# ScalarE writes a residual into PSUM, one block's addition stands first, and GpSimd forms three low parts instead of four

## The chip, the cores and the metric

The kernel runs on one core of a Trainium2 chip. The core has TensorE (matrix products, into PSUM), VectorE and ScalarE (elementwise work, on SBUF and PSUM), GpSimd (elementwise work, on SBUF only), and DMA queues that SyncE and others issue. The metric is the device time of one execution in microseconds; a timed figure is the median of several executions. In the profile the engines are called PE (matmul), PEld (weight load), DVE (VectorE), ACT (ScalarE), POOL (GpSimd) and SP (SyncE); a letter q behind a name is that engine's queue.

## What is computed

One decoder layer in float32 on 256 tokens of width 1024: a mixer of causal pooling and block attention, cross-attention into 256 memory tokens, and a dense SwiGLU layer, each followed by a layer norm over a scaled residual. The change lies in the last step, which is

```
h = layer_norm(DEEPNORM_ALPHA * h + swiglu(h, w_gate, w_up, w_down), ln3_g, ln3_b)

def swiglu(h, w_gate, w_up, w_down):
    return (jax.nn.silu(h @ w_gate) * (h @ w_up)) @ w_down      # w_down: 2816 x 1024

def layer_norm(x, g, b):
    mu = jnp.mean(x, axis=-1, keepdims=True)
    var = jnp.mean(jnp.square(x - mu), axis=-1, keepdims=True)
    return (x - mu) * lax.rsqrt(var + 1e-5) * g + b
```

with DEEPNORM_ALPHA = 2 ** 0.25.

## The kernel before

**High and low parts.** Every float32 operand of a product is split in two: a high part rounded to a format that TensorE takes at full pace (`hi`), and the low part, what is left (`lo = raw - hi`). A product is then three matmuls: high by high, high by low, low by high. For a weight tile of 128x1024, ScalarE makes the high part (a cast) and VectorE the low part (a subtraction of two SBUF tiles). For the tiles whose numbers stand in `ws.helped`, GpSimd makes the low part (line 163).

**The weight stream.** `Stream` holds a list of items in the order in which TensorE uses them. An item is a weight tile from DRAM ("whole"), a pair made from sums of weight blocks ("sums"), or a tile that stands in SBUF already ("home"). Each call of `get` ticks the stream, and a tick prepares at most the next item, up to 9 items (`AHEAD`) past those that TensorE is done with. The order of the items is therefore the order in which casts and low parts enter ScalarE's, VectorE's and GpSimd's queues. Each of these queues runs in order.

**The down projection.** The product with `w_down` is taken in 11 chunks of 256 rows. Ten of them (0 to 9) use a seven-product form for 2x2 blocks: tokens are halved into two blocks of 128, columns into halves of 512, and the 256 rows into two blocks of 128. For these chunks TensorE accumulates

- four shared products `p1`, `p5`, `p6`, `p7`, each in a PSUM bank of its own (`shared_products`);
- products that go straight into the block of the result that needs them: `C11` (token block 0, left half) and `C12` (token block 0, right half) in `four`, and `C21` (token block 1, left half) in `fourth`. The weights of a fourth product are a sum of weight blocks that was put aside earlier in a home of SBUF (`t4`); one home holds the fourth weights of two neighbouring chunks.

Chunk 10 (weight rows 20 and 21, `rest`) is multiplied in the plain way into every block at the end.

The shared products are merged on the way out (`merge`): `merged[0]` is a copy of `p1` by ScalarE (line 1268), and VectorE forms `merged[4] = merged[0] + p6` (line 1269), `merged[1] = merged[4] + p5` for `C12` (1272), `merged[2] = merged[4] + p7` for `C21` (1275) and `merged[3] = merged[2] + p5` for `C22`, token block 1's right half (1278). `C22`, the lower right block, has no straight product; it is `merged[3]`, the residual `ALPHA * h2` and the plain chunk. It is kept in two parts of 256 columns, (1, 512, 768) and (1, 768, 1024), in two banks.

**The end of the kernel.** The function `down` is a generator; each `yield` ends one step of TensorE's work. A dictionary of events puts other engines' work between the steps: at steps 16 to 19 one step each of `merge`. After the last `four`, `down` loads the scale and shift of the last norm (`load_norm`, lines 1290 and 1291), prepares what is left of the stream, and then puts on VectorE's queue, in this order: the two parts of `C22` (line 1299, residual and `merged[3]` in one instruction with two SBUF inputs and a PSUM output), and the addition of `merged[1]` into `C12` (line 1301). TensorE then goes through the pieces: the plain chunk into `C11`, into `C12` (which needs line 1301), into the first part of `C22` (which needs line 1299), then the fourth products of chunks 4 to 7 and 0 to 3 (items 137 to 140, whose low parts GpSimd makes), then the plain chunk into the second part of `C22` and into the two halves of `C21`. For the latter VectorE first adds `merged[2]` (line 1371).

VectorE meanwhile norms token block 0 (lines 1332 to 1351) and begins token block 1. On GpSimd's queue stand, in order, the low parts, the power that makes the reciprocal deviation of token block 0 (line 865), two additions of the shift `b` (line 1350), and the power for token block 1.

**Homes and tags.** The four homes `t4[0]` to `t4[3]` and the norms' buffers come from one pool, in which a tag has a fixed number of slots. Tag `r` has two slots and serves the norms' row buffers; tags `g` and `b` have one slot each and serve the norm's scale and shift. Before, homes 0 and 1 lie in `r`, home 2 in `g`, home 3 in `b`. So the load of the last scale waits until home 2 is split, the load of the last shift until home 3 is, and the last norm's row buffers wait for homes 0 and 1.

Of the kernel before, what the change touches and what calls it, by code (L numbers as in the profile page):

```python
# [11 lines left out]
OP = mybir.AluOpType  # L12
# [3 lines left out]
D = 1024  # L16
# [17 lines left out]
PR_BUFS = 7  # L34
BUSY = 7
SEVEN, LAG, PAIRED, ASIDE = 10, 2, 8, 9
GROUPED = 3


# [171 lines left out]
def decoder_layer(  # L211
# [56 lines left out]
    def row(k):  # L268

        return w_down[k * P:(k + 1) * P].rearrange("(k p) n -> p k n", p=P)  # L270
# [3 lines left out]
    def t4_home(c):  # L274

        if c // 2 not in t4:
            tag, bufs = (("r", 2), ("r", 2), ("g", None), ("b", None))[c // 2]
            t4[c // 2] = nmp.tile([P, 1, D], F32, name=f"t4{c // 2}", tag=tag, **({"bufs": bufs} if bufs else {}))
        return t4[c // 2][:, :, c % 2 * 512:(c % 2 + 1) * 512]

# [17 lines left out]
    def add_low(n):  # L298
        c_low[n] = ws.add(row(2 * n + 1), 1)
# [3 lines left out]
    for n in range(PAIRED):  # L303
        add_low(n)
        if n == 5:
            add_sums(ASIDE)
            add_fourth(ASIDE)
            add_low(ASIDE)
    c_dn = {c: [ws.add(row(2 * c + f), 1) for f in range(2)] for c in range(SEVEN, NFC)}
    for n in (4, 6, 0, 2):  # L310
        add_fourth(n)
    ws.helped.update(c_t4[n][0] for n in (4, 6, 0, 2))


    xt = ap.tile([P, T, D], F32, tag="a8", name="xt")
# [944 lines left out]
    def merge():  # L1260

        p1, p5, p6, p7 = shared

        def u(i):
            return sp.tile([P, 512], F32, name=f"u{i}", tag="pr", bufs=PR_BUFS)

        merged.update({n: u(n) for n in (0, 4)})
        nc.scalar.copy(merged[0], p1)
        nc.vector.tensor_add(merged[4], merged[0], p6)  # L1269
        yield  # L1270
        merged[1] = u(1)
        nc.vector.tensor_add(merged[1], merged[4], p5)  # L1272
        yield
        merged[2] = u(2)
        nc.vector.tensor_add(merged[2], merged[4], p7)  # L1275
        yield
        merged[3] = u(3)
        nc.vector.tensor_add(merged[3], merged[2], p5)  # L1278

    def down():  # L1280

# [13 lines left out]
        acc[1, EDGE, D] = bank("acc")[:, :D - EDGE]  # L1295
        ws.prepare(ws.used + AHEAD)
        ws.held = True
        for c0, c1 in ((512, EDGE), (EDGE, D)):
            nc.vector.scalar_tensor_tensor(acc[1, c0, c1], h2[:, 1, c0:c1], ALPHA, merged[3][:, c0 - 512:c1 - 512],  # L1299
                                           op0=OP.mult, op1=OP.add)  # L1300
        nc.vector.tensor_add(acc[PIECES[1]], merged[1], acc[PIECES[1]])  # L1301
        for piece in (*PIECES[:2], (1, 512, EDGE), (1, EDGE, D), (1, 0, CUT), (1, CUT, 512)):
            t, c0, c1 = piece
            if piece == (1, EDGE, D):
                for c in (4, 6, 0, 2):
                    yield from fourth(c, c + 2)
                yield "left"
            for j, numbers in enumerate(rest):
                y_hi, y_lo = pair(get(done + j), ALL, slice(t * P, (t + 1) * P))
                hi, lo = [w[:, c0:c1] for w in ws.get(numbers, 0)]  # L1310
                end = j == len(rest) - 1
                nc.tensor.matmul(acc[piece], y_hi, hi, start=False, stop=False, skip_group_check=True)  # L1312
                nc.tensor.matmul(acc[piece], y_hi, lo, start=False, stop=False, skip_group_check=True)  # L1313
                nc.tensor.matmul(acc[piece], y_lo, hi, start=False, stop=end, skip_group_check=True)  # L1314
                yield
            yield piece
# [3 lines left out]
        0: lambda: fourth_split(4, PAIRED), 3: lambda: gated_split(ASIDE), 4: lambda: gated_in(NFC - 1),  # L1320
        5: lambda: token_sums_split(ASIDE, aside), 13: lambda: gated_split(NFC - 1),
    }
    events.update({step: lambda: run(parts, 1) for step in (16, 17, 18, 19)})
    for step in range(22):
        events.get(step, lambda: None)()
        run(dn, 1)
# [120 lines left out]
```

## Time and profile before

| | us |
|---|---|
| median of 3 runs | 371.55 |
| lowest, highest | 370.69, 371.56 |
| the profiled execution's own time | 370.8 |
| its span (first to last instruction) | 369.0 |
| TensorE busy | 359.5 (97%) |
| VectorE busy | 316.4 (86%) |
| ScalarE busy | 204.8 (55%) |
| GpSimd busy | 76.8 (21%) |

A timeline row of the profile gives the start and the duration of an instruction in us, the engine, the line of the program, the operation, its output and inputs by the program's names, the shapes, and in brackets how long the engine had been idle and what released it. `w135h` and `w135l` are the high and low part of item 135. A row of several instructions (x2) gives the time from the first one's start to the last one's end. Two instructions of one engine overlap a little, so the distance from start to start is what one of them costs; ends of matmuls are modelled, and their distance from start to start is the better measure.

### The profile page before, as it was taken

The numbers are of one execution on the slowest core, as the hardware profiler recorded it, in microseconds if no ns is written. First come the engines' busy times: TensorE is split into PE (matmuls) and PEld (weight loads), VectorE is DVE, ScalarE is ACT, GpSimd is POOL, SyncE is SP. The second block draws the span as 40 slices with busy tenths as digits, with TensorE's granted clock in tenths as the row PEclk, the third lists the DMA queues.
The fourth block names the chain that finished last, engine by engine and source line by source line (L and its number), as shares of the span: only waits on it lengthen the run. The fifth ranks groups of instructions, "written<-read, shape, count | busy, mean of one in ns | idle before, by whom it ended". The sixth has DMA issues, their size and how long they took to land. (4 is left out here: it accounts for less than half of the span.)

```text
span 369.0 us, 5457 instructions
## 1 busy us (share of the span) xinstructions
PE 359.5 (97%) x1840; PEld 306.6 (83%) x1840; DVE 316.4 (86%) x480; ACT 204.8 (55%) x323; POOL 76.8 (21%) x92
## 2 busy tenths in 40 slices
PE   9999999999999999999999999999999999999495
PEld 8887888888888999988888888888888888888384
DVE  5878999985999888575979989999999999799955
ACT  5867776366342864463164564665475465659211
POOL 1000009200000004300100114422430341210940
PEclk9999999999999999999999999999999999999879
DMA  7996388699936978753009879877986886881311
GB/s 231 417 421 272 116 304 329 188 339 343 363 128 236 398 285 290 254 183 124 0 27 339 290 259 312 282 266 269 324 300 229 326 258 236 267 272 24 111 49 68
DMA packets 35771, 89.75 MB, mean 243 GB/s; under 512 B 4256, under 2 KB 14112, under 8 KB 35616
## 3 DMA queue, kind: packets, MB, share of 16 engines
q1 hardware_dynamic: 34688, 87.57, 67.3%
q0 software_dynamic: 624, 1.57, 1.3%
q8 instruction: 14, 0.23, 0.2%
q10 hardware_dynamic: 432, 0.26, 0.2%
q14 instruction: 13, 0.11, 0.1%
HBM read 82.05 MB, written 7.34 MB: 242 GB/s over the span
## 5 line engine op out<-in xcount | busy, mean ns | idle before, releaser
L1116 POOL TENSOR_TENSOR sraw<-gr 128x128 f32<-128x128 f32 x10 | 8.2, 820 | 103.3 <-DMA gr<-gd 68.9
L865 POOL TENSOR_TENSOR rs<-mv,mhalf 128x1 f32<-128x1 f32 x6 | 4.4, 732 | 71.1 <-DVE mv L863 71.1
L718 POOL TENSOR_TENSOR win<-upad 128x271 f32<-128x271 f32 x4 | 3.5, 881 | 52.7 <-DVE upad L752 52.7
L1117 POOL TENSOR_TENSOR sraw<-sraw,gr 128x128 f32<-128x128 f32 x10 | 12.1, 1212 | 0.8
L493 ACT CAST h2Th<-tp 128x512 fp32r<-128x512 f32 x4 | 2.3, 586 | 14.5 <-PE tp L504 14.5
L1096 ACT ACTIVATE sg<-pg 128x256 f32<-128x256 f32 x22 | 7.9, 380 | 2.8 <-PE pg L391 2.8
L494 DVE TENSOR_TENSOR gTl<-gr,gTh 128x512 fp32r<-128x512 f32 x11 | 8.3, 757 | 0.6 <-ACT gTh L493 0.6
L517 POOL DMA_DIRECT2D xd<-xs x3 | 1.9, 628 | 33.3 <-DVE xs L514 33.3
L1118 POOL TENSOR_TENSOR sraw<-gr 128x128 f32<-128x128 f32 x10 | 8.5, 851 | 0.0
L1097 DVE TENSOR_TENSOR sg<-sg,pg 128x256 f32<-128x256 f32 x22 | 8.4, 415 | 0.1
L525 POOL DMA_DIRECT2D xr<-xd x12 | 6.6, 561 | 8.7 <-DMA xd<-xs 6.4
L493 ACT CAST gTh<-gr 128x512 fp32r<-128x512 f32 x11 | 6.8, 614 | 2.8 <-DMA gr<-gd 2.8
L493 ACT CAST S<-sraw 128x384 fp32r<-128x384 f32 (+1 forms) x10 | 5.3, 533 | 5.3 <-POOL sraw L1118 5.3
L622 ACT ACTIVATE pr<-pr,mx 128x256 f32<-128x256 f32 (+1 forms) x12 | 5.5, 461 | 4.5 <-DVE mx L668 4.5
L622 ACT ACTIVATE xpr<-xs,mx 128x256 f32<-128x256 f32 x8 | 3.7, 470 | 7.4 <-DVE mx L633 7.4
L514 DVE STREAM_TRANSPOSE gs<-sg 128x512 f32<-128x512 f32 x11 | 7.7, 702 | 0.1
L1349 ACT ACTIVATE r<-r,rs 128x512 f32<-128x512 f32 x2 | 1.3, 716 | 11.4 <-POOL rs L865 11.4
L1121 POOL TENSOR_TENSOR S<-gr,sraw 128x128 f32<-128x128 f32 x8 | 7.6, 951 | 0.0
L1312 PE MATMUL acc<-w135h,gTh 128*128 128x256 f32 (+1 forms) x6 | 2.5, 420 | 4.8 <-DVE acc L1301 4.8
L870 DVE SCALAR_TENSOR_TENSOR r<-r,mv,g 128x512 f32<-128x512 f32 (+1 forms) x10 | 7.0, 728 | 0.2
L163 POOL TENSOR_TENSOR w137l<-t,w137h 128x1024 fp32r<-128x1024 f32 x1 | 4.0, 4037 | 14.4 <-ACT w137h L162 14.4
L494 DVE TENSOR_TENSOR S<-sraw,S 128x384 fp32r<-128x384 f32 (+1 forms) x10 | 5.8, 578 | 1.3 <-ACT S L493 1.3
(1400 smaller groups left out, 1436.3 us busy)
## 6 DMA issues: line engine op xcount, KB each, us to landing
gd<-gs SPq DMA_DIRECT2D x11, 256.0 KB, 5.8
gr<-gd SPq DMA_DIRECT2D x44, 64.0 KB, 2.0
pd<-ps SPq DMA_DIRECT2D x4, 384.0 KB, 4.2
pt<-pd SPq DMA_DIRECT2D x16, 96.0 KB, 5.3
g<-in_ln_g SPq DMA_DIRECT2D x3, 512.0 KB, 5.0
b<-in_ln_b SPq DMA_DIRECT2D x3, 512.0 KB, 7.3
wr<-in_w_qkv SPq DMA_DIRECT2D x5, 256.0 KB, 4.7
mr<-in_mem_t SPq DMA_DIRECT2D x1, 1024.0 KB, 11.7
```

The costliest lines, as they stand in the source:

```text
L493: nc.scalar.copy(h, ps)
L494: nc.vector.tensor_sub(l, ps, r32(h))
L514: nc.vector.transpose(st[:, :, at:at + m, :].rearrange("p j m b -> p m j b"), src.rearrange("p m (j b) -> p m j b", b=32))
L525: queue.dma_start(raw[32 * j:32 * (j + 1)].rearrange("p i m b -> p i (m b)"), via[:, j, :].rearrange("(i a) r -> a i r", i=4))
L622: nc.scalar.activation(dst[:, j, :], src[:, j, :], AF.Exp, bias=mx[:, j:j + 1], scale=sign, accum_out=sm[:, j:j + 1])
L870: nc.vector.scalar_tensor_tensor(r, r, self.mv[:, 0:1], gb["g", self.i][:, s], op0=OP.subtract, op1=OP.mult)
L1096: nc.scalar.activation(sg, ps[:, :CW].rearrange("p (f b) -> p f b", f=2), AF.Silu, bias=0.0, scale=1.0)
L1097: nc.vector.tensor_mul(sg, sg, ps[:, CW:].rearrange("p (f b) -> p f b", f=2))
L1116: nc.gpsimd.tensor_add(s1, a21, a22)
L1117: nc.gpsimd.tensor_sub(s2, s1, a11)
L1118: nc.gpsimd.tensor_sub(s3, a11, a21)
L1121: nc.gpsimd.tensor_sub(s4_raw, a12, s2)
```

## The change

Four things change together.

- The homes swap tags: home 0 lies in `b`, home 1 in `r`, home 2 in `g`, home 3 in `r`.
- The stream's order: the fourth weights of chunks 4 and 5 (home 2) come ahead of weight rows 20 and 21, and those of homes 0, 1 and 3 behind them, in this order. Only these three are in `ws.helped`. VectorE makes the low part of the first one.
- The two parts of `C22` no longer come from one fused instruction of VectorE. ScalarE multiplies the residual by ALPHA and writes it into the two banks, and VectorE adds `merged[3]` to each in place.
- VectorE's order: `merged[1]` is added to `C12` first; then `merged[2]` and `merged[3]` are formed (before, at steps 18 and 19), then `merged[3]` is added to the two parts of `C22`. TensorE takes the fourth products of chunks 4 and 5 between the plain chunk into `C12` and that into the first part of `C22`; the other three pairs keep their place ahead of the second part.

```diff
+LATE = 4, 0, 2, 6
...
-            tag, bufs = (("r", 2), ("r", 2), ("g", None), ("b", None))[c // 2]
+            tag, bufs = (("b", None), ("r", 2), ("g", None), ("r", 2))[c // 2]
...
+    add_fourth(LATE[0])
     c_dn = {c: [ws.add(row(2 * c + f), 1) for f in range(2)] for c in range(SEVEN, NFC)}
-    for n in (4, 6, 0, 2):
+    for n in LATE[1:]:
         add_fourth(n)
-    ws.helped.update(c_t4[n][0] for n in (4, 6, 0, 2))
+    ws.helped.update(c_t4[n][0] for n in LATE[1:])
...
         nc.vector.tensor_add(merged[3], merged[2], p5)
+        yield
...
-        for c0, c1 in ((512, EDGE), (EDGE, D)):
-            nc.vector.scalar_tensor_tensor(acc[1, c0, c1], h2[:, 1, c0:c1], ALPHA, merged[3][:, c0 - 512:c1 - 512],
-                                           op0=OP.mult, op1=OP.add)
+        lower = (512, EDGE), (EDGE, D)
+        for c0, c1 in lower:
+            nc.scalar.mul(acc[1, c0, c1], h2[:, 1, c0:c1], ALPHA)
         nc.vector.tensor_add(acc[PIECES[1]], merged[1], acc[PIECES[1]])
+        run(parts, 2)
+        for c0, c1 in lower:
+            nc.vector.tensor_add(acc[1, c0, c1], merged[3][:, c0 - 512:c1 - 512], acc[1, c0, c1])
         for piece in (*PIECES[:2], (1, 512, EDGE), (1, EDGE, D), (1, 0, CUT), (1, CUT, 512)):
             t, c0, c1 = piece
-            if piece == (1, EDGE, D):
-                for c in (4, 6, 0, 2):
-                    yield from fourth(c, c + 2)
+            late = {(1, 512, EDGE): LATE[:1], (1, EDGE, D): LATE[1:]}.get(piece, ())
+            for c in late:
+                yield from fourth(c, c + 2)
+            if len(late) > 1:
                 yield "left"
...
-    events.update({step: lambda: run(parts, 1) for step in (16, 17, 18, 19)})
+    events.update({step: lambda: run(parts, 1) for step in (16, 17)})
```

## The prediction, made before the changed kernel ran

> **What bounds the kernel now.** I read the page first, then the waits of TensorE, then the timelines of the engines in the tail. On the page TensorE is busy for 97% of the 369.0 us span, and the change takes no matmul away, so it can only win or lose TensorE's idle time and its pace. Over the whole run TensorE waits twice (total, count, longest):
>
> ```profile
> PE acc L1312 <- DVE acc L1301: 4.8, 1, 4.8
> PE busy L537 <- PEq L1411: 0.8, 1, 0.8
> ```
>
> The 0.8 us is the start of the program. The other is what the change is about: near the end TensorE stands for the addition into the upper right block (L1301). The timelines of VectorE and of GpSimd, and VectorE's line 1299 alone (shortest, median, longest in ns), show why it is late:
>
> ```profile
> 342.78 0.69 DVE L1269 TENSOR_TENSOR u<-u,x 128x512 f32<-128x512 f32 x1 [0.56 <-ACT u L1268]
> 343.57 0.69 DVE L1272 TENSOR_TENSOR u<-u,x 128x512 f32<-128x512 f32 x1
> 344.17 0.68 DVE L1275 TENSOR_TENSOR u<-u,x 128x512 f32<-128x512 f32 x1
> 344.96 0.69 DVE L1278 TENSOR_TENSOR u<-u,x 128x512 f32<-128x512 f32 x1
> 345.68 3.90 DVE L1299 SCALAR_TENSOR_TENSOR acc<-h,u 128x256 f32<-128x256 f32 x2
> 349.49 0.68 DVE L1301 TENSOR_TENSOR acc<-u,acc 128x512 f32<-128x512 f32 x1
> ```
> ```profile
> 340.45 4.04 POOL L163 TENSOR_TENSOR w137l<-t,w137h 128x1024 fp32r<-128x1024 f32 x1 [14.39 <-ACT w137h L162]
> 344.44 2.37 POOL L163 TENSOR_TENSOR w138l<-t,w138h 128x1024 fp32r<-128x1024 f32 x1
> 346.76 2.53 POOL L163 TENSOR_TENSOR w139l<-t,w139h 128x1024 fp32r<-128x1024 f32 x1
> 349.25 2.54 POOL L163 TENSOR_TENSOR w140l<-t,w140h 128x1024 fp32r<-128x1024 f32 x1
> ```
> ```profile
> L1299 DVE SCALAR_TENSOR_TENSOR acc<-h,u x2: 1416/1990/2564, 345.7 to 347.0; 128x256 f32<-128x256 f32 x2
> ```
>
> The two L1299 end at 347.10 and 349.58, each 0.29 us behind the end of a GpSimd subtraction (346.81 and 349.29). L1299 reads two operands from SBUF, h2 and merged[3]. L1272 to L1278 read one of theirs from PSUM and run 0.69 us while GpSimd is at work. So a VectorE instruction with two SBUF inputs waits out a GpSimd subtraction in flight, and one with a PSUM input does not.
>
> The stall costs more than itself. TensorE's timeline, and two windows (after the busy times of the engines stand the granted clock, the DMA share and GB/s):
>
> ```profile
> 345.05 0.39 PE L1314 MATMUL acc<-w136h,gTl 128*128 128x512 f32 x1
> 350.23 0.79 PE L1312 MATMUL acc<-w135h,gTh 128*128 128x512 f32 x1 [4.80 <-DVE acc L1301]
> ...
> 352.95 0.41 PE L1312 MATMUL acc<-w135h,gTh 128*128 128x256 f32 x1
> ...
> 354.24 0.54 PE L389 MATMUL acc<-w137h,gTh 128*128 128x512 f32 x1
> ...
> 355.07 0.40 PE L389 MATMUL acc<-w137h,gTh 128*128 128x512 f32 x1
> ...
> 359.87 0.28 PE L1312 MATMUL acc<-w135h,gTh 128*128 128x256 f32 x1
> ```
> ```profile
> 347.00:348.00 1.00, 0.00 (x0) 0.00 (x0) 1.00 (x2) 0.00 (x0) 1.00 (x1) 0.85 0.42 168
> 354.00:355.00 1.00, 1.00 (x6) 0.91 (x5) 0.96 (x3) 0.00 (x0) 0.55 (x1) 0.74 0.00 0
> ```
>
> From 355.07 to 359.87 lie 21 matmuls of 512 columns: 0.229 us each. The six before 352.95 took 2.72 us where six at that pace take 1.37; the six of 256 columns took 1.29 against 0.69; the next three 0.83 against 0.69. That is 2.09 us lost after the stall. At half clock within 347 to 348, a mean of 0.85 says that the clock fell at 347.7; by 0.74 it was back at 354.5. So stall and slow clock together cost nearly 7 us.
>
> **The change part by part.** First, what comes ahead of the addition. One low part of 128x1024 (that of fourth product 4) moves from GpSimd to VectorE, and the weight order puts it before rows 20 and 21. VectorE and ScalarE now:
>
> ```profile
> 339.25 1.23 DVE L149 TENSOR_TENSOR w135l<-w133r,w135h 128x1024 fp32r<-128x1024 f32 x1
> 340.38 0.69 DVE L494 TENSOR_TENSOR gTl<-gr,gTh 128x512 fp32r<-128x512 f32 x1
> 340.99 1.23 DVE L149 TENSOR_TENSOR w136l<-w134r,w136h 128x1024 fp32r<-128x1024 f32 x1
> ```
> ```profile
> 340.27 1.04 ACT L162 CAST w138h<-t 128x1024 fp32r<-128x1024 f32 x1
> 341.22 1.05 ACT L162 CAST w139h<-t 128x1024 fp32r<-128x1024 f32 x1
> 342.17 0.57 ACT L1268 COPY u<-x 128x512 f32<-128x512 f32 x1
> 342.65 1.05 ACT L162 CAST w140h<-t 128x1024 fp32r<-128x1024 f32 x1
> ```
>
> VectorE gets a third low part right behind 340.99, at 342.12 (start to start 1.13, as 339.25 to 340.38), ending at 343.35. Its cast is that of slot 137, ahead of the 340.27 row, so it isn't waited for. The idle 0.56 before L1269 hides half of it, and L1269 moves from 342.78 to 343.25. ScalarE makes the same casts in the same order; L1268 is done by 342.74, in time.
>
> Second, the order. L1272 follows L1269 by 0.79, and the addition for the upper right block follows L1272 by the same step for a dependent instruction: 344.04 and 344.83. TensorE starts 0.74 after L1301 does (349.49 to 350.23): 345.57. Its next matmul could have started at 345.05 + 0.23 = 345.28, so a stall of 0.29 us stays. I take no loss of clock for it; the rows bound it between 0 and the 2.09 us of a stall sixteen times as long. TensorE starts this piece 350.23 - 345.57 = 4.66 us earlier and, at full pace, doesn't lose the 2.09.
>
> Third, the residual. Two ScalarE multiplications of 256 columns stand behind the cast that ends at 343.70, and ScalarE is idle then (0.00 in the window above). A PSUM-to-SBUF copy of twice the columns takes 0.57, so I allow 0.6 for both and bound them by 1.2: done by 344.3 to 344.9. They are needed at 347.0: off the path. merged[2] and merged[3] follow the addition at 345.43 (0.60 behind, as 343.57 to 344.17) and 346.22, the two additions at 347.01. Those read PSUM and SBUF, like the pair in the row of 360.07 below (0.76 for two), so GpSimd doesn't hold them, and VectorE is free at 347.71. The piece that needs the first of them is covered: fourth product 4 now stands ahead of it, and TensorE gets there at 345.57 + 2 x 1.37 = 348.31.
>
> Fourth, what is late next. The first GpSimd low part can run once VectorE's third is done (343.35) and ends 2.27 later, as w137l did after w136l (342.22 to 344.49): 345.62. The next end at 347.94 and 350.26 (2.32 apart, 344.49 to 346.81). TensorE needs them at 349.0, 350.4 and 351.8: covered. But token block 0's norm buffer is now the old home of the second of them (L1332 must wait for 347.94), and this is VectorE's tail:
>
> ```profile
> 350.09 0.41 DVE L1332 TENSOR_TENSOR r<-u,acc 128x256 f32<-128x256 f32 x1
> ...
> 351.51 0.43 DVE L856 BATCH_NORM_STATS2 st<-r 128x6 f32<-128x256 f32 x1
> 353.19 0.76 DVE L856 BATCH_NORM_STATS2 st<-acc 128x6 f32<-128x256 f32 x2 [1.25 <-PE acc L1314]
> ...
> 356.17 0.41 DVE L1364 TENSOR_TENSOR r<-acc,g 128x256 f32<-128x256 f32 x1
> 360.07 0.76 DVE L1371 TENSOR_TENSOR acc<-u,acc 128x256 f32<-128x256 f32 x2 [3.48 <-PE acc L391]
> ```
>
> L1332 at 347.98; 1.42 + 0.46 later, without the wait of 1.25, the statistics of the second piece (349.86); 2.98 later L1364 (352.84), done by 353.25. TensorE's last fourth product: 348.31 + 0.69 + 18 x 0.229 = 353.12, against 359.87 now; L1371 follows 0.20 later, at 353.32. So the 3.48 us for which VectorE waited there shrink to under 0.1: it is just in time. From there the order is as before.
>
> The sum: 359.87 - 353.12 = 6.75 (4.66 + 2.09). For the thin margin I keep 6.65. The profiled execution took 370.8 us around its span of 369.0 (1.8 us outside it); less 6.65 it is 364.15. The median of the three timed runs, 371.55, lies 0.75 above it, and as a median is forecast, I give **364.9 us**.
>
> **The rivals.** (a) GpSimd gets there first. Its first low part is released by the cast of 340.27 (ended 341.31), waits for w136l, and when that ends at 342.2 either it or VectorE's third low part goes on. Two readings stand against each other:
>
> ```profile
> 246.50 1.22 DVE L149 TENSOR_TENSOR w92l<-w92r,w92h 128x1024 fp32r<-128x1024 f32 x1
> 247.63 1.49 DVE L149 TENSOR_TENSOR w93l<-w93r,w93h 128x1024 fp32r<-128x1024 f32 x1
> ```
> ```profile
> 246.58 1.46 POOL L1116 TENSOR_TENSOR sraw<-gr 128x128 f32<-128x128 f32 x1 [9.31 <-DVE w91l L149]
> ```
>
> Here GpSimd waited through w92l and then went ahead of w93l, which took 0.27 longer: GpSimd wins the seam. But at 340.45 it waited during gTl, and w136l at 340.99 still ran its plain 1.23: VectorE won, with the very kind of low part that the change uses. If GpSimd wins here, the third low part starts at 344.49 and L1269 at 345.6; L1301 at 347.2, TensorE at 347.9. That is 2.35 later than forecast, a gain of 4.3, less up to 2.1 if the clock falls again: 367.2 to 369.3, likeliest 368.2.
>
> [...]
>
> (b) Slower: the shift b of the last norm arrives late. Its load now waits for the first GpSimd low part (345.62), and on GpSimd's queue the power for token block 1 (L865) stands behind two additions that need b. GpSimd's rows now, and the landing times of these loads (shortest, median, longest in us):
>
> ```profile
> 355.95 2.54 POOL L1350 TENSOR_TENSOR r<-r,b 128x512 f32<-128x512 f32 x2 [1.07 <-ACT r L1349]
> 363.08 0.55 POOL L865 TENSOR_TENSOR rs<-mv,mhalf 128x1 f32<-128x1 f32 x1 [4.59 <-DVE mv L863]
> ```
> ```profile
> DMA to landing us min/median/max: 3.8/6.1/10.5
> ```
>
> Even the longest brings b at 356.1, and the additions end 2.54 later, at 358.7. The result is later than before by 1.1 us only if the power starts after 364.2, so b lands after 361.6, 16 us behind its issue; it would read 372.7. Against it: the longest of these loads took 10.5, and DMA was nearly idle in the windows above (42% and nothing).
>
> (c) The change doesn't do what it says: the addition stays behind something else, most of all VectorE's tail (fourth step). Each 0.1 us that L1332 starts later than 348.1 moves the end by 0.1; with a GpSimd part 1 us slow, 365.8.
>
> **How the numbers follow.** The forecast 0.60, (a) 0.30, (c) 0.07, (b) 0.03. The forecast's own range is 363.8 (fastest run 370.69 less 6.95, no stall left) to 365.7 (0.8 us slip of VectorE's tail or a part of the clock's loss). With (a) the range is **363.8 to 369.3**. A change of 0.3% (1.1 us) is about what a measurement of this kernel can tell from none: faster 0.94, same 0.03, slower 0.03.
>
> **What would show it.** Right: TensorE's wait for the addition is 0.2 to 0.5 us and the clock stays at 1.00 through 345 to 355; the third low part takes 1.23 us at 342.1; the low parts on GpSimd end near 345.6, 347.9 and 350.3; L1371 starts within 0.3 us of the last fourth product's end. Wrong: a third low part of 3 us or more (rival a), a half clock after a short stall, a wait of L1332 for GpSimd past 348.1, or a power of token block 1 that waits for b.

## The result, and the profile after

| | before | after |
|---|---|---|
| median, us | 371.12 (370.37 to 371.56, 4 runs) | 364.86 (364.76 to 365.26, 4 runs) |
| the profiled execution's own time, us | 370.8 | 364.76 |
| its span, us | 369.0 | 363.0 |

The ratio is 0.9835, with a 95% interval of 0.9814 to 0.9856: the change makes the kernel about 6.3 us faster. The forecast was 364.9.

In the kernel after, the addition into the upper right block (L1301 before) is L1304. The merges L1269, L1272, L1275 and L1278 are L1271, L1274, L1277 and L1280; the two parts of the lower right block are L1303 on ScalarE and L1307 on VectorE; L1332 is L1339 and L1371 is L1378. Of TensorE's waits after the change (total, count, longest) the one for the addition:

```profile
PE acc L1319 <- DVE acc L1304: 0.6, 1, 0.6
```

It was 4.8 us. The timelines of VectorE, GpSimd, ScalarE and TensorE after the change show how:

```profile
342.71 1.22 DVE L150 TENSOR_TENSOR w137l<-w134r,w137h 128x1024 fp32r<-128x1024 f32 x1
343.85 0.68 DVE L1271 TENSOR_TENSOR u<-u,x 128x512 f32<-128x512 f32 x1
...
345.42 0.70 DVE L1304 TENSOR_TENSOR acc<-u,acc 128x512 f32<-128x512 f32 x1
...
347.53 0.76 DVE L1307 TENSOR_TENSOR acc<-u,acc 128x256 f32<-128x256 f32 x2
348.20 0.41 DVE L1339 TENSOR_TENSOR r<-u,acc 128x256 f32<-128x256 f32 x1
...
354.05 0.76 DVE L1378 TENSOR_TENSOR acc<-u,acc 128x256 f32<-128x256 f32 x2 [0.70 <-PE acc L393]
```
```profile
341.99 4.19 POOL L164 TENSOR_TENSOR w138l<-t,w138h 128x1024 fp32r<-128x1024 f32 x1 [13.07 <-ACT w138h L163]
346.14 2.40 POOL L164 TENSOR_TENSOR w139l<-t,w139h 128x1024 fp32r<-128x1024 f32 x1
348.50 2.40 POOL L164 TENSOR_TENSOR w140l<-t,w140h 128x1024 fp32r<-128x1024 f32 x1
```
```profile
344.18 0.69 ACT L1303 ACTIVATE acc<-h 128x256 f32<-128x256 f32 x2
```
```profile
345.18 0.39 PE L1321 MATMUL acc<-w137h,gTl 128*128 128x512 f32 x1
346.17 0.50 PE L1319 MATMUL acc<-w136h,gTh 128*128 128x512 f32 x1 [0.60 <-DVE acc L1304]
...
349.03 0.28 PE L1319 MATMUL acc<-w136h,gTh 128*128 128x256 f32 x1
...
353.85 0.28 PE L1319 MATMUL acc<-w136h,gTh 128*128 128x256 f32 x1
```

GpSimd's first low part shows a duration of 4.19 us where the two behind it take 2.40. It ended at 346.18, which is 2.25 us after VectorE's third low part (342.71 + 1.22 = 343.93). So it stood there for the first 1.9 us, and a GpSimd row holds the wait for its turn as well as the work. VectorE's third low part ran its plain 1.22 us although GpSimd had been standing since 341.99: VectorE went ahead at this seam.

The two windows after the change (after the busy times stand the granted clock, the DMA share and GB/s):

```profile
345.00:350.00 5.00, 4.39 (x23) 3.43 (x22) 4.65 (x12) 0.00 (x0) 5.00 (x3) 1.00 0.31 105
350.00:355.00 5.00, 5.00 (x28) 4.30 (x27) 4.19 (x12) 1.54 (x3) 3.74 (x4) 1.00 0.02 9
```

The clock (1.00) no longer falls.

**Where the time went.** The next matmul could have started at 345.18 + 0.23 = 345.41 and started at 346.17. The gap is 0.76 us; before it was 350.23 - 345.28 = 4.95. That gives 4.19 us. The 12 matmuls of 512 columns from 346.17 to 349.03 took 2.86 us where 12 x 0.229 = 2.75 would be full pace: 0.11 us lost against 2.09 before, so 1.98 us come from the clock. TensorE came to this place 0.13 us later (345.18 against 345.05). 4.19 + 1.98 - 0.13 = 6.04, and the last fourth product ends its work 359.87 - 353.85 = 6.02 us earlier. The span is 6.0 us shorter.

### The profile page after: what moved, and what is told of

Read it like the earlier page. It is cut to its first block, busy times and chain, and to the rows that moved or that the text cites. A ratio compares the mean times of both kernels' runs of the same rounds, so it can differ in the third digit from the quotient of the medians.

```text
span 363.0 us, 5459 instructions
## 1 busy us (share of the span) xinstructions
PE 357.3 (98%) x1840; PEld 304.4 (84%) x1840; DVE 314.6 (87%) x481; ACT 205.6 (57%) x325; POOL 73.8 (20%) x91
## 3 DMA queue, kind: packets, MB, share of 16 engines
q0 software_dynamic: 624, 1.57, 1.3%
## 4 chain that ended last, share of the span: by engine, by line
PE 89%; DMA 4%; DVE 3%; SPq 1%; issue 1%; ACT 1%; DVEq 0%
PE pg L391 11%; PE pg L393 11%; PE pg L392 11%; PE pxq L409 6%; PE acc L391 5%; PE acc L392 5%; PE acc L393 5%; PE pxk L435 4%; PE pqk L565 4%; PE pxk L431 2%; PE pu L435 2%; PE xv L393 2%; PE x L391 2%; PE xv L391 2%; PE x L393 2%; PE x L392 2%
## 5 line engine op out<-in xcount | busy, mean ns | idle before, releaser
L1118 POOL TENSOR_TENSOR sraw<-gr 128x128 f32<-128x128 f32 x10 | 6.2, 624 | 106.0 <-DMA gr<-gd 87.7
L1120 POOL TENSOR_TENSOR sraw<-gr 128x128 f32<-128x128 f32 x10 | 11.5, 1146 | 0.0
L1119 POOL TENSOR_TENSOR sraw<-sraw,gr 128x128 f32<-128x128 f32 x10 | 11.2, 1118 | 0.8
L872 DVE SCALAR_TENSOR_TENSOR r<-r,mv,g 128x512 f32<-128x512 f32 (+1 forms) x10 | 7.0, 730 | 0.2
L164 POOL TENSOR_TENSOR w138l<-t,w138h 128x1024 fp32r<-128x1024 f32 x1 | 4.2, 4192 | 13.1 <-ACT w138h L163 13.1
L765 ACT COPY pr<-pxk 128x256 f32<-128x256 f32 x8 | 2.6, 376 | 7.2 <-PE pxk L431 7.2
L858 DVE BATCH_NORM_STATS2 st<-r 128x6 f32<-128x512 f32 (+1 forms) x10 | 6.4, 636 | 0.3
L1001 PE MATMUL xs<-xkTh,xq 128*128 128x256 f32 x32 | 6.4, 283 | 0.0
```

Source lines behind the costliest of these rows:

```text
L1119: nc.gpsimd.tensor_sub(s2, s1, a11)
L1120: nc.gpsimd.tensor_sub(s3, a11, a21)
```

## The experiments

Three things were open. Which of the three parts of the change gives the gain? Why did VectorE go ahead of GpSimd at the seam where rival (a) had 0.30? And from which length does a stall of TensorE cost clock? The kernel before gave medians of 371.64 beside the first four kernels, 371.21 beside the next four (the last of these is the changed kernel once more), and single times of 371.94 and 372.01 beside the last two pairs.

### One part of the change at a time

**The residual alone, on the kernel before.** Four low parts, the old tags and the old order; only the fused instruction is taken apart.

```diff
         for c0, c1 in ((512, EDGE), (EDGE, D)):
-            nc.vector.scalar_tensor_tensor(acc[1, c0, c1], h2[:, 1, c0:c1], ALPHA, merged[3][:, c0 - 512:c1 - 512],
-                                           op0=OP.mult, op1=OP.add)
+            nc.scalar.mul(acc[1, c0, c1], h2[:, 1, c0:c1], ALPHA)
+        for c0, c1 in ((512, EDGE), (EDGE, D)):
+            nc.vector.tensor_add(acc[1, c0, c1], merged[3][:, c0 - 512:c1 - 512], acc[1, c0, c1])
         nc.vector.tensor_add(acc[PIECES[1]], merged[1], acc[PIECES[1]])
```

> Before, with one part of the change alone: ScalarE writes the residual into both banks and VectorE adds merged[3] in place, in the old order (ahead of the addition into C12), four low parts on GpSimd. Port theory (an instruction with two SBUF inputs waits out GpSimd's subtraction, one with a PSUM input doesn't): the two additions take 0.76 us where the fused pair took 3.9, TensorE waits 1.9 us where it waited 4.8; 371.1 less 2.9 to 5.0 (the clock's part) is 366.1 to 368.2. Rival (the wait lies in writing those two PSUM banks or in the length of VectorE's queue, not in the port): the additions take 1.4 us or more each and the time stays above 370.

It took 367.63 us (365.79 to 367.92), ratio 0.9873 [0.9833, 0.9913]. Its VectorE timeline, TensorE's wait and two windows:

```profile
346.18 0.76 DVE L1301 TENSOR_TENSOR acc<-u,acc 128x256 f32<-128x256 f32 x2
346.85 0.69 DVE L1302 TENSOR_TENSOR acc<-u,acc 128x512 f32<-128x512 f32 x1
```
```profile
PE acc L1313 <- DVE acc L1302: 2.0, 1, 2.0
```
```profile
345.00:350.00 5.00, 2.99 (x9) 2.10 (x8) 3.98 (x10) 0.00 (x0) 5.00 (x3) 0.79 0.62 198
350.00:355.00 5.00, 5.00 (x23) 4.25 (x23) 3.52 (x8) 1.54 (x3) 4.16 (x4) 0.87 0.03 11
```

GpSimd is busy in the whole first window, and still the two additions of `merged[3]` take 0.76 us together where the fused pair took 3.90. So the additions, which read one operand from PSUM, weren't held by GpSimd, while the pair with two SBUF inputs was. No run shows what in the chip makes the difference; the port of the expectations' "port theory" was the author's assumption. TensorE still stood for 2.0 us, since the addition it waits for stood last, and that stall cost clock: 0.79 and 0.87.

**The order alone, on the kernel before.** The fused pair stays on VectorE, but behind the addition into the upper right block.

```diff
         nc.vector.tensor_add(merged[3], merged[2], p5)
+        yield
...
+        nc.vector.tensor_add(acc[PIECES[1]], merged[1], acc[PIECES[1]])
+        run(parts, 2)
         for c0, c1 in ((512, EDGE), (EDGE, D)):
             nc.vector.scalar_tensor_tensor(acc[1, c0, c1], h2[:, 1, c0:c1], ALPHA, merged[3][:, c0 - 512:c1 - 512],
                                            op0=OP.mult, op1=OP.add)
-        nc.vector.tensor_add(acc[PIECES[1]], merged[1], acc[PIECES[1]])
...
-    events.update({step: lambda: run(parts, 1) for step in (16, 17, 18, 19)})
+    events.update({step: lambda: run(parts, 1) for step in (16, 17)})
```

> Before, with only VectorE's order changed: the addition into C12 right behind merged[1], then merged[2], merged[3] and the two fused instructions. Theory: TensorE waits 0.3 us or less ahead of the upper right block; the fused pair still waits for GpSimd (ends near 347.1 and 349.6), which costs TensorE some 0.5 us ahead of the first part of C22 and makes VectorE's tail late by about 1.2 us. Gain 4.95 + 2.09 - 1.7 = 5.3: 365.8. Rival (the residual on ScalarE carries the gain): less than 3 us gained, above 368.

It took 365.7 us (365.54 to 365.83), ratio 0.9831 [0.9792, 0.9869]: nearly all of the gain. VectorE's timeline and TensorE's waits:

```profile
344.79 0.70 DVE L1299 TENSOR_TENSOR acc<-u,acc 128x512 f32<-128x512 f32 x1
...
346.83 3.25 DVE L1302 SCALAR_TENSOR_TENSOR acc<-h,u 128x256 f32<-128x256 f32 x2
```
```profile
PE acc L1314 <- DVE acc L1373: 0.7, 1, 0.7
PE acc L1314 <- DVE acc L1302: 0.5, 1, 0.5
```

The fused pair still waits for GpSimd (3.25 us), but now only 0.5 us of it reaches TensorE. The other 0.7 us come near the end of TensorE's work, where VectorE's tail, pushed back by the fused pair, is late with line 1373 (L1371 before). Neither stall cost clock: it stayed at 1.00 from 345 to 360 us.

**Three low parts, the new tags and the new order of weights, with VectorE's old order and the fused pair.** The kernel after, with those lines of it put back; the fourth products of chunks 4 and 5 keep their new place too.

```diff
-        lower = (512, EDGE), (EDGE, D)
-        for c0, c1 in lower:
-            nc.scalar.mul(acc[1, c0, c1], h2[:, 1, c0:c1], ALPHA)
+        for c0, c1 in ((512, EDGE), (EDGE, D)):
+            nc.vector.scalar_tensor_tensor(acc[1, c0, c1], h2[:, 1, c0:c1], ALPHA, merged[3][:, c0 - 512:c1 - 512],
+                                           op0=OP.mult, op1=OP.add)
         nc.vector.tensor_add(acc[PIECES[1]], merged[1], acc[PIECES[1]])
-        run(parts, 2)
-        for c0, c1 in lower:
-            nc.vector.tensor_add(acc[1, c0, c1], merged[3][:, c0 - 512:c1 - 512], acc[1, c0, c1])
...
-    events.update({step: lambda: run(parts, 1) for step in (16, 17)})
+    events.update({step: lambda: run(parts, 1) for step in (16, 17, 18, 19)})
```

> After, with VectorE's old order and the fused instructions (three low parts on GpSimd, new order of weights, tags and fourth products stay). Port theory: the fused pair waits for the ends of GpSimd's second and third low part (near 348.5 and 350.8), the addition into C12 comes at about 351.1 and TensorE waits 6 us or more; 371 to 373, no gain over before. Rival (the fewer low parts on GpSimd or the moved fourth product carry a good part of the gain): under 369.

It took 372.77 us (371.14 to 373.72), ratio 1.002 [1.0, 1.004]: nothing is gained. TensorE's wait, the fused pair and two windows:

```profile
PE acc L1316 <- DVE acc L1304: 6.1, 1, 6.1
```
```profile
346.04 4.50 DVE L1302 SCALAR_TENSOR_TENSOR acc<-h,u 128x256 f32<-128x256 f32 x2
```
```profile
345.00:350.00 5.00, 0.06 (x1) 0.00 (x0) 4.86 (x4) 0.00 (x0) 5.00 (x3) 0.72 0.27 105
350.00:355.00 5.00, 3.80 (x11) 3.04 (x12) 3.61 (x10) 0.00 (x0) 0.25 (x1) 0.60 0.00 0
```

The fused pair waits out two GpSimd subtractions (they end at 347.77 and 350.26, the pair at 350.54), now for 4.50 us, and TensorE stands for 6.1 us. One low part less on GpSimd didn't free VectorE, because the three that are left follow each other without a gap (they start at 341.28, 345.44 and 347.74, and take 4.20, 2.33 and 2.52 us).

**Four low parts, with everything else of the change.** This is the remaining part of the change taken back by itself.

```diff
-    ws.helped.update(c_t4[n][0] for n in LATE[1:])
+    ws.helped.update(c_t4[n][0] for n in LATE)
```

> After, with the fourth low part back on GpSimd (all four there). VectorE is 1.13 us freer ahead of the addition into C12. If VectorE wins the seams between its low parts as it did twice against GpSimd's first subtraction: TensorE's wait falls from 0.6 to 0.3 us or less, GpSimd's last low part ends near 352 and holds VectorE's centring of token block 0 for up to 1 us; 364.4 to 365.2. If GpSimd wins a seam: a VectorE low part takes 3.4 us, the wait is near 2 us, 366 to 367.5.

It took 364.54 us (364.36 to 364.76), ratio 0.98 [0.9768, 0.9833]; the interval overlaps that of the changed kernel, so the two can't be told apart. GpSimd's first low part and one VectorE instruction of the tail:

```profile
338.19 6.46 POOL L164 TENSOR_TENSOR w135l<-t,w135h 128x1024 fp32r<-128x1024 f32 x1 [10.83 <-ACT w135h L163]
```
```profile
350.15 2.14 DVE L872 SCALAR_TENSOR_TENSOR r<-r,mv,g 128x512 f32<-128x512 f32 x1
```

GpSimd stood here through four VectorE instructions in a row (w134l, gTl, w136l and w137l) and lost every seam. The price of the fourth low part comes later: L872 has two SBUF inputs and waits for the last low part on GpSimd, which ends at 351.74; it takes 2.14 us where the kernel after takes 0.77. VectorE's tail is then later, but TensorE waits only 0.3 us for it.

**The waiting instruction put second.** On the four low parts, L872 changes places with the instruction behind it, which reads PSUM.

```diff
-    norm.centre(0, 512)
     centre(norm, 512, D, acc[PIECES[1]])
+    norm.centre(0, 512)
```

> Four low parts on GpSimd, and in token block 0's norm VectorE centres the right half first (its product stands in PSUM), then the left half (two SBUF inputs). In the kernel with four low parts alone the left half's centring took 2.14 us, because it waited for GpSimd's last low part, and TensorE then waited 0.3 us near the end. Port theory: the wait is spent on the right half's centring, the left half's takes 0.7 to 1.7 us, VectorE is 0.4 us earlier, TensorE no longer waits: 0.2 to 0.4 us under the kernel with four low parts, 364.2. Rival (TensorE's remaining waits hang on something else): no difference.

It took 364.92 us (364.27 to 365.2), ratio 0.9825 [0.9803, 0.9846]. The changed kernel, run again beside it, took 364.93 (364.55 to 365.43), ratio 0.9829 [0.9808, 0.985].

> The changed kernel once more, on the same chip as the other three, so that they can be compared: 364.9, and 0.3 to 0.7 us above the version with four low parts and the right half centred first.

VectorE's and GpSimd's timelines with the two exchanged:

```profile
351.17 0.75 DVE L1347 SCALAR_TENSOR_TENSOR r<-acc,mv,g 128x512 f32<-128x512 f32 x1
351.83 1.42 DVE L872 SCALAR_TENSOR_TENSOR r<-r,mv,g 128x512 f32<-128x512 f32 x1
```
```profile
350.30 2.40 POOL L164 TENSOR_TENSOR w140l<-t,w140h 128x1024 fp32r<-128x1024 f32 x1
```

These rows also answer a rival that the residual alone leaves open, since there the kind of instruction changed together with the place of its operand. L1347 is of the same kind as L872 and as the fused pair, but reads `acc` from PSUM: it took its plain time (0.75 us; 0.74 in the kernel after) while GpSimd was at work on `w140l`. L872, right behind it, reads SBUF twice and was held (1.42 us against 0.77). So here the place of the operand decided, not the kind of instruction.

The wait of L872 is shorter by half (1.42 - 0.77 = 0.65 us against 1.37), and TensorE's wait for the tail is gone, but the time doesn't show it: the 0.2 to 0.4 us that were expected didn't come, and the runs don't show why. No version beats the changed kernel by more than can be measured.

**What follows for the parts.** The order alone gives 5.9 us (371.64 - 365.7), the residual alone 4.0, and the two aren't added: each takes the fused pair from the path between `merged[1]` and TensorE. The order takes it away whole; the residual leaves its two short additions and two merges in front. With the order in place, another 1.2 us come (365.7 against 364.54 with four low parts). They match the two waits of 0.5 and 0.7 us that the fused pair leaves with the order alone, but the residual, the new tags, the new order of weights and the moved fourth products were not told apart here. Without VectorE's new order and the residual, the rest of the change gained nothing (372.77), and the count of low parts makes no difference that these runs can tell.

### Who goes ahead at a seam

A seam is the place where one VectorE instruction with two SBUF inputs ends, another follows back to back, and a GpSimd instruction stands ready. Either VectorE goes on, and the GpSimd row grows (6.46 us for 2.40 in the run above), or GpSimd goes first, and the second VectorE row grows (`w93l` in the kernel before, 1.49 us for 1.22). Theories: the size of GpSimd's instruction decides; or the type of its output; or where its operands come from; or the place in VectorE's stream. All six kernels tried here have four low parts on GpSimd, as in the run above; of their edits the lines that matter are shown, and those that allocate a spare tile are left out.

**Size.** On the kernel with four low parts, GpSimd's first low part is cut into 128 and 896 columns; in another, GpSimd makes 128 columns of the item before, whose rest VectorE makes.

```diff
-                (nc.gpsimd if i in self.helped else nc.vector).tensor_sub(lo[:, :, s], raw, r32(hi[:, :, s]))
+                cuts = [slice(0, 128), slice(128, raw.shape[2])] if i == min(self.helped, default=-1) else [s]
+                for c in cuts:
+                    (nc.gpsimd if i in self.helped else nc.vector).tensor_sub(lo[:, :, c], raw[:, :, c], r32(hi[:, :, c]))
```
```diff
+                if i + 1 == min(self.helped, default=-1):
+                    nc.gpsimd.tensor_sub(lo[:, :, :128], raw[:, :, :128], r32(hi[:, :, :128]))
+                    subs = [slice(128, raw.shape[2])]
                 for s in subs:
                     nc.vector.tensor_sub(lo[:, :, s], raw[:, :, s], r32(hi[:, :, s]))
```

> Four low parts on GpSimd, the first of them in two instructions, 128 and then 896 columns. Whole, it waited from 338.2 through four VectorE instructions with two SBUF inputs (to 342.4) and lost three seams between them. Theory size (a short GpSimd instruction gets the seam, a long one doesn't): the 128 columns end within 1.5 us of their start and the VectorE instruction behind that seam takes 0.27 us longer; the 896 columns wait for VectorE's gap near 342.4. Theory kind (GpSimd's subtraction of this output type comes late after its idle time): the 128 columns wait for the gap too, 4 us or more. Theory issue order: both go ahead at their next seam, and a VectorE low part takes 3 us or more. Only in the last is the time above 365.5.

> Four low parts on GpSimd, and GpSimd also makes 128 columns of the low part just ahead of them (VectorE the other 896). So GpSimd has run an instruction of the same kind within 1 us of the first long one. Theory size: the 128 columns get a seam, the long one behind still waits for the gap near 342.4. Theory kind or first use: once the 128 columns have run, the long one gets the next seam, and a VectorE low part takes 3 us or more; TensorE then waits 1 to 3 us for the addition into C12 and the time is 366 or more.

They took 364.9 and 365.15 us (one run each). GpSimd's timeline of the second:

```profile
337.70 5.31 POOL L150 TENSOR_TENSOR w134l<-w132r,w134h 128x128 fp32r<-128x128 f32 x1 [8.76 <-DVE w132l L153]
```

An instruction of 128 columns stood for 5.31 us here and lost four seams. In the first kernel the two pieces take 6.59 us together, and VectorE's rows beside them keep their plain length (1.22 us, and 0.68 for gTl). Size didn't decide.

**Output type.** An extra GpSimd subtraction of 32 columns whose result nobody reads, with a plain float32 output, and the same with the rounded output that a low part has.

```diff
+                if i + 1 == min(self.helped, default=-1):
+                    nc.gpsimd.tensor_sub(self.spare, raw[:, 0, :32], r32(hi[:, 0, :32]))
```
```diff
-                    nc.gpsimd.tensor_sub(self.spare, raw[:, 0, :32], r32(hi[:, 0, :32]))
+                    nc.gpsimd.tensor_sub(self.spare.bitcast(F32R), raw[:, 0, :32], r32(hi[:, 0, :32]))
```

> Four low parts on GpSimd, and ahead of them GpSimd subtracts 32 columns of the tile before (its raw and its high part) into a spare tile, result unused, written as float32. It stands near 337.5 among VectorE's back-to-back instructions with two SBUF inputs. Theory output type (a subtraction that writes the rounded format loses every seam, one that writes float32 gets the next, as the ten sums of the token blocks did): it ends within 1.5 us, and the VectorE instruction behind that seam takes 0.1 to 0.3 us longer. Rival place or first use (here GpSimd loses whatever it writes): it ends only in VectorE's gap near 342.5, after 4 us or more. Time 364.5 to 365.5 either way.

> The same with the spare tile written in the rounded format, nothing else different. Theory output type: it ends only in VectorE's gap near 342.5, after 4 us or more. Rival place or first use: the same as the run with float32, whichever that is. Time 364.5 to 365.5.

They took 364.79 and 364.76 us (one run each). GpSimd's timeline of the first:

```profile
337.39 5.24 POOL L152 TENSOR_TENSOR warm<-w132r,w134h 128x32 f32<-128x32 f32 x1 [8.75 <-DVE w132l L150]
```

It lost its seams, and with the rounded output the row reads 5.24 us as well. The type of the output didn't decide.

**Operands, and place.** Earlier in the run GpSimd wins its seams with subtractions that work on the tokens' sums (the seam of `w93l` is one). So the same 32 columns (results unread) were tried in two ways: on the weights' operands, but at ten places through the run, nine of them early; and on the sums' operands, but late, as GpSimd's first instruction in the last stretch.

```diff
+                if i in (79, 80, 92, 93, 103, 104, 105, 116, 127, 134):
+                    nc.gpsimd.tensor_sub(self.spare, raw[:, 0, :32], r32(hi[:, 0, :32]))
```
```diff
-        5: lambda: token_sums_split(ASIDE, aside), 13: lambda: gated_split(NFC - 1),
+        5: lambda: (token_sums_split(ASIDE, aside), nc.gpsimd.tensor_sub(
+            ws.spare, s_raw[ASIDE][:, 0, 0, :], r32(aside[0][:, 0, :32]))), 13: lambda: gated_split(NFC - 1),
```

> Four low parts on GpSimd, and ten times GpSimd subtracts 32 columns of a weight tile and its high part into a spare float32 tile, result unused: nine times in the chunk loop (220 to 327 us), where its token sums got every seam against VectorE's low parts, and once near 337.5. Theory operands: the nine lose their seams too, and end only in a gap of VectorE, while the token sums beside them go on winning. Theory place: the nine win the next seam (1.5 us or less each), the last one loses four as before. Time 364.5 to 366.

> Four low parts on GpSimd, and GpSimd subtracts 32 columns of a token sum and its high part (the tiles of the sums, not a weight tile) into a spare float32 tile, result unused. It starts near 335.5, among VectorE's back-to-back instructions with two SBUF inputs (335.4 to 342.4). Theory operands (what is read from a weight tile and its high part loses every seam): it ends within 1.5 us and the VectorE instruction behind its seam is 0.1 to 0.3 us longer. Theory place (in this stretch GpSimd loses whatever it reads): it ends near 342.5, 7 us after its start. Time 364.5 to 365.5.

The first took 364.91 us. Its GpSimd and VectorE timelines:

```profile
246.03 0.74 POOL L152 TENSOR_TENSOR warm<-w92r,w92h 128x32 f32<-128x32 f32 x1 [8.69 <-ACT w92h L148]
...
337.58 5.19 POOL L152 TENSOR_TENSOR warm<-w132r,w134h 128x32 f32<-128x32 f32 x1 [8.81 <-DVE w132l L150]
```
```profile
246.57 1.28 DVE L150 TENSOR_TENSOR w92l<-w92r,w92h 128x1024 fp32r<-128x1024 f32 x1
```

On weight operands GpSimd went first at 246.5 (0.74 us; w92l took 1.28 where its plain time is 1.22), and with the same instruction at 337.58 it stood for 5.19 us. Of the nine early ones six went first at a seam, two met no seam, and one came 0.05 us before its seam and stood through one VectorE instruction (1.29 us). With the same operands the place made the difference.

The second took **373.4 us** (one run), 8.6 us more than its twins at 364.8. GpSimd's and VectorE's timelines, TensorE's waits and three windows:

```profile
334.25 0.60 POOL L1329 TENSOR_TENSOR warm<-sraw,S 128x32 f32<-128x32 f32 x1 [7.04 <-ACT S L495]
```
```profile
334.66 0.74 DVE L164 TENSOR_TENSOR w131l<-w129r,w131h 128x512 fp32r<-128x512 f32 x1
...
338.19 3.43 DVE L150 TENSOR_TENSOR w134l<-w132r,w134h 128x1024 fp32r<-128x1024 f32 x1
341.55 2.90 DVE L496 TENSOR_TENSOR gTl<-gr,gTh 128x512 fp32r<-128x512 f32 x1
344.37 3.35 DVE L150 TENSOR_TENSOR w136l<-w133r,w136h 128x1024 fp32r<-128x1024 f32 x1
347.64 3.37 DVE L150 TENSOR_TENSOR w137l<-w134r,w137h 128x1024 fp32r<-128x1024 f32 x1
```
```profile
PE acc L1321 <- DVE w136l L150: 3.7, 1, 3.7
PE acc L1321 <- DVE w137l L150: 1.6, 1, 1.6
PE acc L1320 <- DVE acc L1305: 1.0, 1, 1.0
```
```profile
345.00:350.00 5.00, 1.65 (x3) 0.83 (x3) 5.00 (x2) 0.00 (x0) 4.93 (x2) 0.63 0.28 99
350.00:355.00 5.00, 2.94 (x6) 1.93 (x7) 4.62 (x8) 0.00 (x0) 0.00 (x0) 0.50 0.00 0
355.00:360.00 5.00, 5.00 (x23) 4.08 (x23) 4.79 (x14) 0.98 (x2) 0.72 (x2) 0.85 0.00 0
```

The spare instruction went first at its seam, as the theory of operands had it and against the theory of place. But it also stood there 3 us earlier than the spare ones above, at 334.25 instead of 337.4. It cost VectorE 0.06 us (w131l 0.74 instead of 0.68). Having got in once, GpSimd went first at each of the next four seams where it stood ready: w134l, w136l and w137l take 3.4 us instead of 1.22, gTl 2.90 instead of 0.68. GpSimd's instructions there are the low parts themselves, and at these seams they lost in the other kernels. So neither the operands nor the place alone decided. TensorE stands for 6.3 us in three pieces, and the clock is low for most of 15 us (0.63, 0.50 and 0.85). This is rival (a) come true, four times over.

All seams of the 14 traces (before, after, and the twelve runs above) between two `TENSOR_TENSOR` rows, where GpSimd had been standing for 0.2 us or more when the first row ended, counted by whether the second row is more than 0.03 us longer than its kind usually is. A chain is an unbroken run of VectorE instructions with two SBUF inputs:

| where in VectorE's chain | GpSimd first | VectorE first |
|---|---|---|
| first to fourth instruction | 207 | 0 |
| eighth or later, GpSimd not yet in this chain | 0 | 31 |
| eighth or later, GpSimd got in at the fourth (the run of 373.4) | 4 | 0 |

Of the 207, 205 lie behind the first or second instruction of a chain. Where GpSimd had come less than 0.2 us before the seam, young chains are mixed (9 times GpSimd first, 13 times VectorE).

What fits all 242 is history: in these traces GpSimd went first while VectorE's chain was young (207 of 207), and in the one long chain into which it had got it kept its turn (4 of 4); against a long chain in which it had had no turn it got none from the eighth instruction on (0 of 31). This was made to fit after the runs. The part on keeping the turn rests on four seams of one execution, and all seams from the eighth on lie in the same stretch of the program. What in the chip carries it isn't shown, nor what happens between the fifth and the seventh instruction, where no trace has a seam. GpSimd's idle time alone isn't it: in young chains its subtractions won after up to 9.7 us of idleness too. But in the long chain a turn and a short idle time come together (GpSimd won after 3.2 us of idleness or less, and lost after 8.7 us or more), and no run tells these two apart.

### What a stall costs in clock

No run was made for this alone; the runs above give the series. The time at half clock is worked out from the two or three windows of 5 us of each run: (1 - granted clock) x 5 / 0.5, summed. The 0.5 stands for the lowest clock that a window here shows: 0.50 from 350 to 355 us in the run of 373.4, and in each window of 1 us from 348 to 354 in the kernel before.

| kernel | TensorE's stall, us | time at half clock, us |
|---|---|---|
| four low parts | 0.3 | 0 |
| after | 0.6 | 0 |
| order alone | 0.5 and 0.7 | 0 |
| residual alone | 2.0 | 2.1 + 1.3 = 3.4 |
| before | 4.8 | 2.3 + 4.5 = 6.8 |
| three low parts, fused pair | 6.1 | 2.8 + 4.0 = 6.8 |
| sums' operands late | 3.7, 1.6 and 1.0 | 3.7 + 5.0 + 1.5 = 10.2 |

The times that aren't 0 read 3.4, 6.8, 6.8 and 10.2 us: one, two, two and three times 3.4. What sets this step isn't shown. In the traces a stall of up to 0.7 us cost none and one of 2.0 us cost one step; between them nothing was measured. One of the four timed executions of the residual alone took 365.79 us where the others took 367.52 to 367.92, and its mean granted clock was 0.999 where theirs was 0.994. So this kernel lost clock in three executions and next to none in the fourth. Why isn't shown: the stall of that execution wasn't traced.

## Why the prediction was right

**What bounds the kernel: right.** The stall for the addition and the clock after it were the whole matter: 4.19 + 1.98 of the 6.02 us. The ScalarE residual alone and the order alone show the cause too: with GpSimd at work the fused pair took 3.25 us in its new place, and the two additions with a PSUM operand took 0.76.

**Step 1, the third low part: right in form, 0.6 us late.** It took 1.22 us, in the place forecast and ahead of GpSimd, but at 342.71 rather than 342.12. VectorE came into the stretch later, as the same instruction in both timelines shows, before and after:

```profile
335.84 1.22 DVE L149 TENSOR_TENSOR w132l<-w130r,w132h 128x1024 fp32r<-128x1024 f32 x1
```
```profile
336.43 1.22 DVE L150 TENSOR_TENSOR w132l<-w130r,w132h 128x1024 fp32r<-128x1024 f32 x1
```

Over the 14 traces this row starts between 335.7 and 337.0, and TensorE moves with it only in part: its first matmul on that tile follows 3.5 to 4.0 us behind (339.83 before, 339.96 after). The forecast took one trace's start of VectorE as fixed, and so the 4.66 us of the earlier start came out as 4.19.

**Step 2, the order: right.** From L1271 to L1304 lie 1.57 us (forecast 1.58), from L1304 to TensorE 0.75 (0.74). All three stand 0.6 late with step 1, and TensorE's gap was 0.76 where 0.29 was left. Of the clock's 2.09 us, 1.98 came back; the choice to charge no clock for the short stall held (1.00).

**Step 3, the residual: right.** Both multiplications took 0.69 us (0.6 allowed, 1.2 the bound) and were done at 344.87, ahead of the additions at 347.53. These took 0.76 as forecast. The row of 360.07, on which the forecast leaned here, couldn't show that GpSimd doesn't hold them, since GpSimd was idle then; the residual alone shows it (0.76 us with GpSimd busy throughout).

**Step 4, what is late next: wrong in its reason, without effect on the time.** The prediction had L1332 (now L1339) wait for the second low part on GpSimd, since token block 0's norm buffer was the old home. L1339 started at 348.20, right behind the additions, and that low part ended only at 348.54. There is no such dependence, and the sentence in the description above that the last norm's row buffers wait for homes 0 and 1 is wrong as well. The class `Norm` gives the last norm another buffer:

```python
            if i < 3:
                self.r = nmp.tile([P, D], F32, name="r", bufs=2)
            else:
                self.r = sp.tile([P, D], F32, name="r3", tag="pair", bufs=3)
```

VectorE's tail so came only 0.1 us later than forecast (L1371 ended at 353.35, not 353.25), while TensorE came 0.7 us later (353.85, not 353.12): VectorE waited 0.70 us for TensorE ahead of L1378, where under 0.1 was forecast. L1378 still came 0.20 us behind the start of the plain chunk (354.05 against 353.85), the distance forecast, since TensorE set it. The low parts on GpSimd ended at 346.18, 348.54 and 350.90, each 0.6 us later than forecast with VectorE's third one, and TensorE waited for none.

**Rival (a) had the wrong odds and the wrong price.** VectorE won this seam, and all 31 of its kind. The two readings weighed against each other in the prediction were no contradiction: the row of 246.58 stands early in a chain and that of 340.45 late in one. Had this seam gone as that of 246.58 did, GpSimd, standing since 341.99, would have gone ahead of the low part of 342.71; it didn't. In the 207 seams of young chains it did. Where the rival came true, in one run of a kernel with four low parts, it cost 8.6 us and not 2.3 to 4.4 (367.2 to 369.3 less 364.9), because GpSimd went first at every following seam and not at one, with 10.2 us of half clock behind it.

**Rivals (b) and (c)** did not come: TensorE waited for neither the tail nor the shift, and the power of token block 1 on GpSimd waited for VectorE alone (1.83 us, for L865).

**The sum.** The forecast gain was 6.65 us and the profiled gain 6.0 (370.8 - 364.76). Between the medians it is 371.12 - 364.86 = 6.26, so 0.39 less than forecast. The forecast was still met to 0.04, because its base, the median of three runs, 371.55, lies 0.43 above the median with one run more. Two small misses cancel, and that the median was met so closely is luck: for the profiled execution the sum gave 364.15, and 364.76 was measured. The mis-sized term is the first one, 4.66 for 4.19.

## What to carry to other kernels

When a consumer of one engine waits behind a group of instructions on another, put what it needs first; that alone gave 5.9 us here, where the whole change gave 6.3, and taking the slow instruction apart without moving it gave 4.0. While GpSimd works, give VectorE instructions a PSUM operand where one is to be had, since those didn't wait (0.76 us for a pair against 3.25 to 4.50). Judge a TensorE stall by the clock it costs too: here a stall of up to 0.7 us was only itself, one of 2.0 us came with 3.4 us at half clock in the traced execution, and those of 4.8 and 6.1 us came with 6.8 us.

## What the hardware showed that was not expected

- Who goes ahead at a seam went with the history of VectorE's chain, not with the size, output type or operands of GpSimd's instruction: 207 to 0 for GpSimd in the first four instructions, 31 to 0 for VectorE from the eighth on where GpSimd had had no turn. In one run a single GpSimd instruction of 32 columns, let in at the fourth, came with four later seams turned over, and the kernel took 373.4 us instead of 364.8.
- A GpSimd row in the trace includes its wait for a turn: 6.46 us for a low part that runs in 2.40, 5.24 us for 32 columns.
- The time at half clock behind TensorE's stalls came in steps in the seven kernels compared: 0, 3.4, 6.8 and 10.2 us.
